# HGRN2 heads on one Trainium2 core: eight strip products in four runs of two levels instead of three runs of three, two and three

## The chip, the core and the metric

The kernel runs on one core of one Trainium2 chip. The core has a matmul engine (PE; its weight loads are shown as an engine of their own, PEld), three other computing engines (DVE, ACT, POOL), a queue engine (SP), an on-chip memory, and PSUM, eight banks into which PE writes and from which DVE and ACT read. Each engine works through its instructions in order and waits on semaphores for the others. The metric is the device time in microseconds (us) of one execution; three were run, and their median is the time before.

## What is computed

A backbone of two layers over 1024 latent tokens and 256 context tokens, width 1024, float32. The first layer (neighbourhood attention beside an mLSTM) is not touched. The second has 16 bidirectional HGRN2 heads with key and value width 128. Cut to what matters here, a head computes, in each direction:

```python
def step(S, xs):
    qc, kc, vc, lfc = xs
    b = jnp.cumsum(lfc, axis=2)
    o = jnp.einsum('bhtk,bhkv->bhtv', qc * jnp.exp(b), S)
    pair = jnp.exp(jnp.where(tri, b[:, :, :, None, :] - b[:, :, None, :, :], -jnp.inf))
    a = jnp.einsum('bhtk,bhtsk->bhts', qc, pair * kc[:, :, None, :, :])
    o = o + jnp.einsum('bhts,bhsv->bhtv', a, vc)
    ...
    S = jnp.exp(bL[:, :, 0])[..., None] * S + jnp.einsum('bhsk,bhsv->bhkv', kc * jnp.exp(bL - b), vc)
    return S, o
```

Here q = silu(projection), f = lb + (1 - lb) * sigmoid(projection) for each direction, k = 1 - f and lf = log(f); the state S starts from the context tokens. The outputs of the two directions are added, normalised, gated and projected.

## The kernel before

**A head.** The 1024 tokens are cut into 8 chunks of 128. Within a chunk the scores a (128 x 128, both directions at once, `gA`) are not computed with the decay between every pair of tokens, but in levels. Level 0 to 6 pairs neighbouring blocks of h = 1, 2, 4 ... 64 tokens. K (`gK`) and Q (`gQ`), both 128 x 2 x 1024, start as 1 - f and q * f, and after each level `hg_update` (line 1299) multiplies half of each in place with the block totals (`gT`), four DVE instructions of 128 x 512 at L1312, so that K is decayed to the border of the next larger block and Q from it; L1315 forms the next totals. The product of a level is thus a plain matmul, of which only the places that belong to the level are kept. One more level, called None, is the diagonal: (K0 + K1) against q.

**Strips.** `hg_level` (line 1276) computes a level as 32 products: for each of 8 chunks and 4 strips of 32 rows, 32 x 32 results (level 6: 32 x 64) on a quarter of the matmul array (`tile_position=(0, r)`, line 1295). Each call makes two matmuls and two weight loads in the trace, so a level is 64 matmul rows. `hg_pick` (line 1260) is a copy on ACT that gathers every other block of K or Q into a contiguous `gksel` tile (four buffers); where a level does not pick Q, the strips read Q in place through a strided view.

**Runs.** `hg_burst` (line 1266) issues a list of levels. It raises their priority by 3000, and binds each further level behind the first matmul of the first one (`issue_after`, which adds an order on one engine). Nothing binds the first level: it goes as soon as its operands and banks allow. The runs are (1, 0, None), then (3, 2), then (6, 4, 5): 192, 128 and 192 matmuls. DVE merges levels 0, None and 1 to 4 into `gA32` (L1215, and masked copies at L1214), ACT copies `gA32`, level 5 and level 6 into `gA` (L1237 to L1240).

**The order of the work.** The instruction order of each engine is planned when the kernel is built, by priority (order of the program text) and by when operands and banks are free in a planned time line. In the program text, `hg_intra` (line 1179) for head h has eight slots, filled by the loop at lines 1633 to 1646: the scan of head h-1 (`hg_scan`, line 1318: `back` in slots 0 to 2, `ahead` in slots 3 to 6), the projections of head h+1 (`hg_parts`, line 821: f of direction 0 in slots 2 and 3, of direction 1 in 4 and 5, q in 6 and 7), its context state (`hg_ctx`, slot 1), the load of v and the output of head h-2. A projection of 512 tokens is 24 matmuls of 128 x 512 (lines 127 to 129, `dense`), into one of two `mm` banks that ACT empties.

**Banks.** In this stage PSUM has `mm` (2), `tr` (2, transposes), `s` (3) and `acc` (1). The strips and the state matmuls both use `s`: each of a head's 14 states (L1327, read by DVE at L1329) and two context states (L1173, read by DVE at L1175) takes a tile there, and so does each pair of levels (level 6 and level 1 one each).

## Time and profile before

| | |
|---|---|
| three runs | 3323.93 us median, 3320.77 to 3324.95 |
| the profiled execution | 3323.42 us, its span 3321.6 us |
| PE busy | 3265.4 us (98%), 29504 matmuls |
| DVE, ACT, POOL busy | 2201.2, 1551.6, 499.4 us |
| the HGRN2 heads | first strip matmul at 2200.7 us, last at 3167.9 us |
| strip matmuls (L1295) | 8192 |

The profile is one execution, recorded by the hardware. A row names the source line, the engine, the operation, what is written and read by the program's names, and the shape. Matmuls overlap, and the end of one is modelled: start to start is the true pace, and a row's duration is longer. Idle time before an instruction is put down to what released it; "issue" means that the profile shows nothing that it waited for. The granted clock is the share of its full clock that PE was allowed.

### The profile page before, as it was taken

The page shows a single profiled execution, that of the slowest core. Times are in us where ns is not written, and L with a number is a line of the kernel's source. Part 1 is how long each engine was busy: PE and PEld are TensorE (multiplying, and loading weights), DVE is VectorE, ACT ScalarE, POOL GpSimd, SP SyncE. Part 2 cuts the span into 40 slices and gives each one's busy share as a digit, 9 for nine tenths or more (in the row PEclk, how much of TensorE's full clock was granted, in tenths as well). Part 3 has the DMA queues.
Part 4 walks back from the last instruction along what each step waited for, and adds up shares of the span by engine and source line. Part 5 has one row for each costly group of instructions (what it writes and reads, how often), then busy time and mean ns, then how long its engine had stood idle before and what let it go on. Part 6 is the DMA issues. An engine that isn't in the chain of part 4 may idle for free. (4 is left out here: it accounts for less than half of the span.)

```text
span 3321.6 us, 73610 instructions
## 1 busy us (share of the span) xinstructions
PE 3265.4 (98%) x29504; PEld 2909.4 (88%) x29504; DVE 2201.2 (66%) x5071; ACT 1551.6 (47%) x3469; POOL 499.4 (15%) x834
## 2 busy tenths in 40 slices
PE   8999999999999999999999999999999999999999
PEld 5689999999999999888877999888888888888887
DVE  5578747766667654666767766657767767767745
ACT  5322145555455534556645433355555555555541
POOL 3111112222222211121222111100000000000010
PEclk9999999999999999999999999999999999999999
DMA  8543322322232224455567333221122122122345
GB/s 270 199 140 103 120 80 55 95 74 80 77 84 79 80 89 134 142 169 155 153 196 225 115 105 108 91 66 55 56 65 62 56 65 65 53 65 65 119 159 171
DMA packets 359559, 360.36 MB, mean 108 GB/s; under 512 B 30584, under 2 KB 304184, under 8 KB 359088
## 3 DMA queue, kind: packets, MB, share of 16 engines
q1 hardware_dynamic: 315248, 246.36, 25.3%
q0 software_dynamic: 43824, 109.16, 9.7%
q8 instruction: 232, 3.80, 0.5%
q14 instruction: 111, 0.91, 0.1%
q10 hardware_dynamic: 144, 0.13, 0.0%
HBM read 271.98 MB, written 83.42 MB: 107 GB/s over the span
## 5 line engine op out<-in xcount | busy, mean ns | idle before, releaser
L127 PE MATMUL mm<-hh,wh 128*128 128x512 f32 (+1 forms) x1564 | 568.6, 364 | 0.1
L129 PE MATMUL mm<-hh,wl 128*128 128x512 f32 (+1 forms) x1564 | 561.7, 360 | 1.8 <-DVE wl L75 1.8
L128 PE MATMUL mm<-hl,wh 128*128 128x512 f32 (+1 forms) x1564 | 562.1, 359 | 0.0
L127 PE MATMUL mm<-wh,hh 128*128 128x256 f32 x1880 | 541.6, 289 | 3.7 <-ACT wh L74 3.6
L128 PE MATMUL mm<-wl,hh 128*128 128x256 f32 x1880 | 541.9, 289 | 0.1
L129 PE MATMUL mm<-wh,hl 128*128 128x256 f32 x1880 | 541.8, 289 | 0.2 <-DVE hl L75 0.2
L127 PEld LDWEIGHTS mm<-wh,hh 128*128 128x128 f32 x1880 | 358.0, 191 | 6.2 <-ACT wh L74 3.8
L128 PEld LDWEIGHTS mm<-wl,hh 128*128 128x128 f32 x1880 | 358.5, 191 | 3.6 <-issue 1.7
L129 PEld LDWEIGHTS mm<-wh,hl 128*128 128x128 f32 x1880 | 358.4, 191 | 3.3 <-issue 1.5
L127 PEld LDWEIGHTS mm<-hh,wh 128*128 128x128 f32 x1564 | 296.6, 190 | 43.3 <-issue 4.2
L129 PEld LDWEIGHTS mm<-hh,wl 128*128 128x128 f32 x1564 | 295.9, 189 | 43.3 <-DVE wl L75 2.0
L128 PEld LDWEIGHTS mm<-hl,wh 128*128 128x128 f32 x1564 | 296.7, 190 | 42.1 <-issue 4.2
L74 ACT CAST wh<-wraw 128x512 fp32r<-128x512 f32 x292 | 177.9, 620 | 209.9 <-PE mm L128 97.2
L75 DVE TENSOR_TENSOR wl<-wraw,wh 128x512 fp32r<-128x512 f32 x292 | 197.7, 687 | 84.2 <-ACT wh L74 69.8
L774 PE MATMUL mm<-woh,yh 128*128 128x512 f32 (+1 forms) x420 | 167.8, 399 | 4.1 <-ACT yh L74 3.1
L776 PE MATMUL mm<-woh,yl 128*128 128x512 f32 (+1 forms) x420 | 167.3, 399 | 0.5 <-DVE yl L75 0.4
L775 PE MATMUL mm<-wol,yh 128*128 128x512 f32 (+1 forms) x420 | 164.9, 393 | 0.0
L1312 DVE TENSOR_TENSOR gQ<-gQ,gT 128x512 f32<-128x512 f32 x192 | 123.9, 687 | 61.4 <-PE s L1295 60.3
L74 ACT CAST wh<-b 128x512 fp32r<-128x512 f32 x122 | 75.5, 620 | 178.6 <-PE sa L129 62.6
L1312 DVE TENSOR_TENSOR gK<-gK,gT 128x512 f32<-128x512 f32 x192 | 123.5, 685 | 12.3 <-PE s L1295 8.5
L1263 ACT COPY gksel<-gK 128x1024 f32<-128x1024 f32 x96 | 110.9, 1155 | 29.4 <-PE s L1295 15.1
L152 POOL TENSOR_SCALAR gss<-gss 128x4 f32<-128x4 f32 x32 | 12.9, 402 | 721.0 <-ACT gon L1353 721.0
(595 smaller groups left out, 7856.3 us busy)
## 6 DMA issues: line engine op xcount, KB each, us to landing
wraw<-in_wc_dram SPq DMA_DIRECT2D x130, 256.0 KB
wraw<-yd SPq DMA_DIRECT2D x116, 256.0 KB
wraw<-in_wab_dram SPq DMA_DIRECT2D x98, 256.0 KB
md<-ev POOLq DMA_DIRECT2D x78, 256.0 KB, 2.8
adar<-in_wada_dram POOLq DMA_DIRECT2D x16, 1024.0 KB, 5.9
b<-in_wc_dram SPq DMA_DIRECT2D x62, 256.0 KB
adar<-in_wada_dram SPq DMA_DIRECT2D x16, 512.0 KB
wraw<-in_wab_dram SPq DMA_DIRECT2D x64, 128.0 KB
```

Source lines behind the costliest of these rows:

```text
L74: nc.scalar.copy(hi, x)
L75: nc.vector.tensor_tensor(out=lo, in0=x, in1=hi.bitcast(F32), op=ALU.subtract)
L127: mm(ps, lhsT=lh(k), rhs=rh(k), start=(first and k == 0), stop=False)
L128: mm(ps, lhsT=lh(k), rhs=rl(k), start=False, stop=False)
L129: mm(ps, lhsT=ll(k), rhs=rh(k), start=False, stop=(last and k == nk - 1))
L152: g.tensor_scalar(out=out, in0=ssq, scalar1=mul, scalar2=EPS, op0=ALU.mult, op1=ALU.add)
L774: mm(ps, lhsT=yh[:, k, :], rhs=w.h(k)[:, cols], start=(k == 0), stop=False)
L775: mm(ps, lhsT=yh[:, k, :], rhs=w.l(k)[:, cols], start=False, stop=False)
L776: mm(ps, lhsT=yl[:, k, :], rhs=w.h(k)[:, cols], start=False, stop=(k == 7))
L1263: self.nc.scalar.copy(o.rearrange("p (b s i) -> p b s i", s=2, i=h), self.hg_view(t, h))
L1312: nc.vector.tensor_tensor(out=t[:, i, :, s, :], in0=t[:, i, :, s, :], in1=bc(tot), op=ALU.mult)
```

## The change

`hg_intra` issues four runs of two levels: (0, None) behind slot 2, (2, 1) behind slot 4, (4, 3) behind slot 6 and (6, 5) behind slot 7, so 128 matmuls each. Level 0's run no longer holds level 1, which was the only level of it that read Q in place; of the pairs (2, 1), (4, 3) and (6, 5) the first member reads Q in place (level 6 K too) and the second reads picked copies. Q is picked for levels 0, 1, 3 and 5 instead of 0, 2, 4 and 5, K for levels 0 to 5 as before. Slot 7 moves from behind the copies into `gA` to ahead of the last run. `dense` notes the last projection matmul written so far (`self.last_pe`), and `hg_burst` now binds the first level too: behind that matmul. The strips get a tile of their own, `sb`, of two banks and one buffer, and `s` shrinks from three banks to one, for the states alone.

```diff
--- before.py
+++ after.py
@@ -126,7 +126,7 @@
         for k in range(nk):
             mm(ps, lhsT=lh(k), rhs=rh(k), start=(first and k == 0), stop=False)
             mm(ps, lhsT=lh(k), rhs=rl(k), start=False, stop=False)
-            mm(ps, lhsT=ll(k), rhs=rh(k), start=False, stop=(last and k == nk - 1))
+            self.last_pe = mm(ps, lhsT=ll(k), rhs=rh(k), start=False, stop=(last and k == nk - 1))
 
 
     def proj_nat(self, ps, w, tt, c0, n, k0=0, nk=KD):
@@ -1192,53 +1192,58 @@
             for part in slots[i]:
                 part()
 
-        def two(w=32):
-            ps = self.ps("s", [P, 512])
-            return [ps[:, i : i + 8 * w].rearrange("p (c i) -> p c i", i=w) for i in range(0, 512, 8 * w)]
-
+        def banks(n):
+            ps = self.t(self.pp, [P, 1024], F32, "sb")
+            return [ps[:, i : i + 256].rearrange("p (c i) -> p c i", i=32) for i in range(0, n * 256, 256)], ps[:, 512:]
+
+        bc = lambda m: m.unsqueeze(1).to_broadcast([P, 8, 32])
+        put = lambda lev, ps: nc.vector.copy_predicated(A32, bc(self.lmask[:, lev - 1, :]), ps)
+        pick = lambda t, lev: self.hg_pick(t, lev, pool)
         slot(0)
-        k0, q0 = self.hg_pick(K, 0, pool), self.hg_pick(Q, 0, pool)
+        k0, q0 = pick(K, 0), pick(Q, 0)
         ks = self.hg_tile(pool)
         nc.vector.tensor_tensor(out=ks, in0=K[:, 0, :], in1=K[:, 1, :], op=ALU.add)
         self.hg_update(H, 0, pool)
-        k1 = self.hg_pick(K, 1, pool)
+        k1 = pick(K, 1)
         slot(1)
         slot(2)
-        (p0, pd), (p1, _) = two(), two()
-        self.hg_burst([(1, p1, k1, Q), (0, p0, k0, q0), (None, pd, ks, q)])
+        (p0, pd), _ = banks(2)
+        self.hg_burst([(0, p0, k0, q0), (None, pd, ks, q)])
+        q1 = pick(Q, 1)
         self.hg_update(H, 1, pool)
-        k2, q2 = self.hg_pick(K, 2, pool), self.hg_pick(Q, 2, pool)
-        self.hg_update(H, 2, pool)
-        k3 = self.hg_pick(K, 3, pool)
-        bc = lambda m: m.unsqueeze(1).to_broadcast([P, 8, 32])
-        put = lambda m, ps: nc.vector.copy_predicated(A32, bc(m), ps)
+        k2 = pick(K, 2)
         nc.vector.tensor_tensor(out=A32, in0=p0, in1=bc(self.lmask0), op=ALU.mult)
-        put(self.ident8, pd)
-        put(self.lmask[:, 0, :], p1)
+        nc.vector.copy_predicated(A32, bc(self.ident8), pd)
         slot(3)
         slot(4)
-        p2, p3 = two()
-        self.hg_burst([(3, p3, k3, Q), (2, p2, k2, q2)])
+        (p1, p2), _ = banks(2)
+        self.hg_burst([(2, p2, k2, Q), (1, p1, k1, q1)])
+        self.hg_update(H, 2, pool)
+        k3, q3 = pick(K, 3), pick(Q, 3)
         self.hg_update(H, 3, pool)
-        k4, q4 = self.hg_pick(K, 4, pool), self.hg_pick(Q, 4, pool)
-        self.hg_update(H, 4, pool)
-        k5, q5 = self.hg_pick(K, 5, pool), self.hg_pick(Q, 5, pool)
-        self.hg_update(H, 5, pool)
-        put(self.lmask[:, 1, :], p2)
-        put(self.lmask[:, 2, :], p3)
+        k4 = pick(K, 4)
+        put(1, p1)
+        put(2, p2)
         slot(5)
         slot(6)
-        (p4, p5), (p6,) = two(), two(64)
-        self.hg_burst([(6, p6, K, Q), (4, p4, k4, q4), (5, p5, k5, q5)])
+        (p3, p4), _ = banks(2)
+        self.hg_burst([(4, p4, k4, Q), (3, p3, k3, q3)])
+        self.hg_update(H, 4, pool)
+        k5, q5 = pick(K, 5), pick(Q, 5)
+        self.hg_update(H, 5, pool)
+        put(3, p3)
+        put(4, p4)
+        slot(7)
+        (p5,), p6 = banks(1)
+        p6 = p6.rearrange("p (c i) -> p c i", i=64)
+        self.hg_burst([(6, p6, K, Q), (5, p5, k5, q5)])
         self.hg_update(H, 6, pool)
-        put(self.lmask[:, 3, :], p4)
         for r in range(0, P, 32):
             s, o = slice(r, r + 32), r ^ 32
             nc.scalar.copy(A[s, :, s], A32[s])
             nc.scalar.copy(A[s, :, o : o + 32], p5[s])
         for r in (0, 64):
             nc.scalar.copy(A[r : r + 64, :, 64 - r : 128 - r], p6[r : r + 64])
-        slot(7)
         H["kn"] = {}
         for hf in (1, 0):
             for d in range(2):
@@ -1265,12 +1270,12 @@
 
     def hg_burst(self, todo):
         tc = self.tc
-        first, p = None, tc.cur_priority
+        first, p = self.last_pe, tc.cur_priority
         tc.cur_priority = p - 3000
         for lev, ps, k, q in todo:
-            with tc.issue_after(first.ins) if first else nullcontext():
+            with tc.issue_after(first.ins):
                 m = self.hg_level(lev, ps, k, q)
-            first = first or m
+            first = m if first is self.last_pe else first
         tc.cur_priority = p
 
     def hg_level(self, lev, ps, k, q):
@@ -1625,7 +1630,7 @@
                 self.rawp = pool
                 self.zero = self.t(pool, [P, CTX], F32, "gzero", 1)
                 nc.vector.memset(self.zero, 0.0)
-                l1.enter_context(self.pp.phase(s=3, acc=1))
+                l1.enter_context(self.pp.phase(s=1, sb=(1, 2), acc=1))
                 st, parts = self.hg_parts(0, pool, early)
                 for part in sum(parts, []):
                     part()
@@ -1720,7 +1725,7 @@
     @contextmanager
     def phase(self, **tags):
         with self.tc.tile_pool(name="ps" + "".join(tags), bufs=1, space=PSUM) as pool:
-            self.inner = {t: (pool, n) for t, n in tags.items()}
+            self.inner = {t: (pool, n if isinstance(n, int) else n[0]) for t, n in tags.items()}
             yield
         self.inner = {}
```

## The prediction

> **What bounds the kernel now.** I read the page first (engines, clock, queues), then the busy time stretch by stretch from one head's first strip run to the next, then PE's rows in order of time, then the waits.

> ```profile
> span 3321.6 us, 73610 instructions
> PE 3265.4 (98%) x29504; PEld 2909.4 (88%) x29504; DVE 2201.2 (66%) x5071; ACT 1551.6 (47%) x3469; POOL 499.4 (15%) x834
> q8 instruction: 232, 3.80, 0.5%
> ```

> PE is busy 98% of the span, so only time in which PE stands, or PE work itself, is worth anything. The third line is a DMA queue that carries instructions: 3.80 MB in 232 packets, 16.4 KB each. PE's two rows count 59,008 instructions; over 232 packets that is 254 a packet. So PE's program is brought in by blocks of some 255 instructions, about 128 pairs of a weight load and a matmul.

> Now the HGRN2 heads. Each stretch runs from the first strip run of a head to that of the next (columns: length, then busy time and instructions of PE, PEld, DVE, ACT, POOL, granted clock, DMA share, GB/s).

> ```profile
> 2316.58:2380.78 64.20, 62.00 (x843) 54.60 (x843) 43.64 (x83) 32.60 (x64) 4.01 (x6) 0.97 0.20 59
> 2380.78:2441.17 60.39, 60.39 (x843) 53.09 (x842) 43.20 (x83) 32.63 (x64) 4.05 (x6) 1.00 0.21 63
> 2441.17:2502.24 61.07, 60.59 (x843) 53.18 (x843) 43.29 (x83) 32.70 (x64) 4.04 (x6) 1.00 0.21 62
> 2502.24:2566.88 64.64, 62.14 (x843) 54.58 (x843) 43.62 (x83) 32.62 (x64) 4.02 (x6) 0.97 0.19 55
> 2627.27:2689.99 62.72, 60.59 (x843) 53.19 (x842) 43.41 (x83) 32.61 (x64) 4.05 (x6) 1.00 0.20 61
> 2750.39:2812.69 62.30, 60.57 (x843) 53.18 (x842) 43.43 (x83) 32.61 (x64) 4.02 (x6) 1.00 0.21 61
> 2812.69:2875.09 62.40, 60.56 (x843) 53.17 (x842) 43.45 (x83) 32.62 (x64) 4.02 (x6) 1.00 0.20 61
> 2935.49:2998.07 62.58, 60.59 (x844) 53.19 (x843) 43.40 (x83) 32.62 (x64) 4.04 (x6) 1.00 0.20 61
> 2998.07:3058.46 60.39, 60.39 (x843) 53.11 (x843) 43.23 (x83) 32.63 (x64) 4.05 (x6) 1.00 0.21 63
> ```

> The same 843 matmuls take 60.39 us in some heads, with PE busy throughout, and 61 to 65 us in others. A clean head leaves PE no idle time and DVE and ACT much (43 and 33 of 60 us). What the others lose is in PE's rows (start, duration, name, count, and in brackets the idle time before it and what ended it):

> ```profile
> 2320.38 0.65 PE L1295 MATMUL s<-gq,gksel 128*32 128x32 f32 x31 [2.20 <-issue]
> 2443.06 0.67 PE L1295 MATMUL s<-gq,gksel 128*32 128x32 f32 x54 [0.48 <-issue]
> 2506.60 0.22 PE L1295 MATMUL s<-gq,gksel 128*32 128x32 f32 x1 [2.50 <-issue]
> 2631.09 0.40 PE L1295 MATMUL s<-gq,gksel 128*32 128x32 f32 x24 [2.13 <-issue]
> 2753.57 0.62 PE L1295 MATMUL s<-gq,gksel 128*32 128x32 f32 x47 [1.73 <-issue]
> 2817.17 0.27 PE L1327 MATMUL s<-gv,gkn 128*128 128x128 f32 x1 [1.84 <-issue]
> 2939.21 0.35 PE L1295 MATMUL s<-gq,gksel 128*32 128x32 f32 x18 [1.99 <-issue]
> 3062.35 0.57 PE L1295 MATMUL s<-gq,gksel 128*32 128x32 f32 x41 [2.38 <-issue]
> 3133.82 0.38 PE L1346 MATMUL acc<-gS,gQ 128*128 128x128 f32 x1 [1.71 <-issue]
> ```

> Nine stops, ended by "issue": no semaphore explains them, and PE has no others of that kind between 2190 and 3200 us. Seven lie in the last third of a head's first strip run (the level that reads gq, matmuls 129 to 192 of it), two a few matmuls behind that run. Where they lie is regular: 31 matmuls are left after the stop in one head and 54 two heads later; 1, 24, 47 in heads two apart; 18 and 41. That is 23 a step. A head holds 843 + 842 = 1685 instructions with rows; two heads 3370 = 13 blocks of 256 + 42, or 21 pairs, and 23 if each head has two instructions without rows. So I read each stop as PE reaching the edge of a block that has not come yet.

> **Part by part: the runs.** Two runs of the old kernel, with what surrounds them:

> ```profile
> 2405.18 0.39 PE L127 MATMUL mm<-hh,wh 128*128 128x512 f32 x1
> 2405.41 0.39 PE L128 MATMUL mm<-hl,wh 128*128 128x512 f32 x1
> 2405.73 1.10 PE L1295 MATMUL s<-gQ,gK 128*32 128x64 f32 x64
> 2406.76 0.49 PE L1345 MATMUL acc<-gv,gA 128*128 128x128 f32 x2
> 2407.08 0.39 PE L1346 MATMUL acc<-gS,gQ 128*128 128x128 f32 x2
> 2407.31 0.39 PE L1347 MATMUL acc<-gS,gQ 128*128 128x128 f32 x2
> ...
> 2413.90 0.39 PE L128 MATMUL mm<-hl,wh 128*128 128x512 f32 x1
> 2414.21 1.30 PE L1295 MATMUL s<-gksel,gksel 128*32 128x32 f32 x128
> 2415.44 0.49 PE L1347 MATMUL acc<-gS,gQ 128*128 128x128 f32 x2
> ```

> A projection matmul starts 0.23 us after the one before, a pair on acc takes 0.23, but 128 strip matmuls pass in 1.23 us, under 10 ns each. A block whose 128 pairs all lie inside a strip run is used up in 1.2 us. By the stops, fetching one takes longer: 1.2 us plus a stop of up to 2.5, so some 3.5 to 4 us, with one block fetched ahead. A run of 192 can hold a whole block for 64 of 128 alignments, and a few more where the edge falls just behind it: nine of sixteen heads stopped. A run of 128 can hold a whole block at one alignment only; else part of the block is projections or acc pairs, of which ten to twenty add the missing 2.5 us. The old kernel shows it: its second run (128) in sixteen heads and, in all but the first head, its last (128) make 31 runs, at alignments that go round in steps of 23 pairs per two heads, and none has a stop. The change makes all four runs 128.

> What is removed: seven heads above exceed 60.39 by 3.81, 0.68, 4.25, 2.33, 1.91, 2.01 and 2.19 us, 17.2 in all. In two of them the granted clock is 0.97, and the head loses some 1.5 us more than the stop: PE was slowed after it. The last two heads run beside output matmuls, so I take their stops, 2.38 and 1.71 plus 0.2 each (by which the excess of 2.33 or 2.19 stands above the idle time shown, 2.13 and 1.99): 4.5. Sum 21.7 us.

> What is added: a run costs 0.09 us at its entry (0.32 instead of 0.23 from the matmul before) and about 0.25 at its end (the 64 above take 1.03 us, 0.15 more than 63 steps of 14 ns; the acc pair behind them 0.32 instead of 0.23). But in fifteen heads the old third run (64 + 128) came apart, as shown, so they have four runs already. Only the first head gains one: 0.3 us. In all 21.4 us are gained.

> **The other parts.** The number of strip matmuls, picks, updates, masked copies and states is the same; q1 and q3 are picked instead of q2 and q4, ten picks a head as before, on ACT, which has 27 us a head to spare. The first run no longer reads Q in place, so the second update need not wait for it:

> ```profile
> DVE gQ L1312 <- PE s L1295: 60.3, 16, 4.3
> DVE gS L1329 <- PE s L1327: 37.8, 50, 2.3
> PEld s L1295 <- DVE gS L1329: 0.4, 1, 0.4
> ```

> That wait of DVE, 3.8 us a head, is cover and no cost: PE was busy beside it. I take nothing for it. A fixed place moves runs later than their operands allow; then DVE's updates wait longer, with 17 us a head to spare. If that is used up, PE would stand at the next run. Slot 7, now ahead of the last run, holds 24 projection matmuls (5.5 us at 0.23), the sigmoid and product behind them on ACT and DVE, and the last two chunks on acc with their squares on ACT and their root on POOL; it issues no DMA (q's weights are fetched from slot 6). So update 6, the copies into gA and the next states come up to 5.5 us later; the next head's context and f projections (24 matmuls of 0.12 and 24 of 0.23, 8.4 us) cover that, and without them it would cost 5.5 us a head. I take zero.

> The disputed part is the state matmul's bank. "s" shrinks from three banks to one, and sixteen tiles a head (fourteen states, two context states) pass through it, each held until DVE has read it:

> ```profile
> 2423.62 0.83 PE L1327 MATMUL s<-gv,gkn 128*128 128x128 f32 x6
> 2430.73 0.34 DVE L1329 SCALAR_TENSOR_TENSOR gS<-gS,gT,s 128x128 f32<-128x128 f32 x1
> 2440.62 0.38 PE L1327 MATMUL s<-gv,gkn 128*128 128x128 f32 x2
> 2441.04 0.35 DVE L1329 SCALAR_TENSOR_TENSOR gS<-gS,gT,s 128x128 f32<-128x128 f32 x1 [0.87 <-PE s L1327]
> ```

> The first two rows: three states go out at once and the last is read 7 us later; that needs three banks. The last two: one tile from start to free in 0.77 us. Sixteen at 0.77 take 12 of 60 us, so one bank suffices if DVE answers soon. Behind a waiting state matmul PE's whole queue stands. Bounds: nothing, if projections are always placed between two states, as around 2440; or 0.77 - 0.23 = 0.54 us for each of 16 x 16 tiles, 138 us, if they follow each other bare. The nearest row is the third wait above: in this stage PE waited for a state's reading once, 0.4 us, though the banks were shared with the strips. The order is planned with these waits, so I take the lower end, zero, and keep up to 0.5 us a head (8 us) in the range. Nothing below zero: a clean head has no idle PE to win.

> Sum: 3323.4 us of the profiled execution (its span of 3321.6 and 1.8 around it) - 21.7 + 0.3 = 3302.0; the median of the three runs (3323.9) is 0.5 above that execution: I forecast 3302.5.

> **Rivals.** *Slower: the single bank.* PE's matmuls stand behind a state whose bank DVE has not read, because DVE is inside an update:

> ```profile
> L1312 DVE TENSOR_TENSOR gQ<-gQ,gT 128x512 f32<-128x512 f32 x192 | 123.9, 687 | 61.4 <-PE s L1295 60.3
> ```

> Twelve of them a head, 0.69 us each. Break-even is 21.4/16 = 1.3 us a head, two such waits; with four of sixteen tiles waiting 0.69 us it is 2.8 us a head, 44 in all: 3323.9 - 21.4 + 44 = 3347. For it: DVE answered up to 7 us late. Against it: no PE wait on DVE now, projections at hand everywhere. Chance 0.13.

> *No change: the stops are not the runs' length.* If the blocks come late for another reason, the stops move to other places and remain: 3324. [...] Against this rival stands that PE's other runs, of 128 and less, never stop this way. Chance 0.09.

> *Half the gain: a run of 128 may fall just on a block.* Four runs in sixteen heads are 64; if one in eight is aligned so and loses 1.3 us, 10 us come back: 3313. Chance 0.1.

> **How the numbers follow.** The forecast has 0.68, the half gain 0.1, no change 0.09, the bank 0.13. A measurement of this kernel can tell about 0.2%, 6.6 us. Faster by more than that: 0.68 and nearly all of the 0.1, less a little for waits of the bank that eat the gain: 0.76. Within: 0.11. Slower: 0.13. The forecast's own range is 3297 to 3311: below, if the reordered end also loses this wait for the first output matmul (2 us, and 1.5 for a slower clock behind it), less 2 us for the scatter of runs (3320.8 to 3325.0);

> ```profile
> 3107.93 0.50 PE L774 MATMUL mm<-wh,yh 128*128 128x512 f32 x1 [2.07 <-ACT yh L74]
> ```

> above, with 0.5 us a head for the bank. To leave out no more than 2 in 10 the range reaches over the half gain and no change: 3297 to 3325.

> **What would show it.** Right: every head some 60.4 us apart, no idle time ended by "issue" at L1295 or just behind, four rows x128 a head (one of them 64 + 64 where widths differ), granted clock 1.00 throughout. Wrong: "issue" stops inside runs of 128 (the half gain), or as many elsewhere (no change); "PE s L1327 <- DVE gS L1329" among the waits with more than 20 us (the bank); runs split into 64s, at 0.3 us each.

## The result, and the profile after

The changed kernel takes 3442.05 us (median of four, 3439.7 to 3448.3) against 3324.4 for the kernel before: a ratio of 1.0362, with an interval of 1.035 to 1.0375 (the two medians alone give 1.0354). It is slower by 118 us, where 21 us less were forecast. The page of the changed kernel:

```profile
span 3441.9 us, 73572 instructions
PE 3324.7 (97%) x29504; PEld 2959.2 (86%) x29504; DVE 2209.4 (64%) x5071; ACT 1551.1 (45%) x3469; POOL 507.8 (15%) x834
core 0: 3441.9 us, clock 0.976
```

The last of these lines (from the view of cores) is the mean granted clock, 0.995 before. The span is 120 us longer. PE's matmuls are the same 29504, but PE stands 117 us instead of 56 (span less busy time), and is busy 59 us longer with the same work. Both arise from the first strip run on: behind it PE stands 86 us instead of 24, and ahead of it about as long as before (31.5 and 32.5 us). Two heads, from first strip run to first strip run, and then one border between heads cut in three (columns as in the prediction):

```profile
2664.35:2733.76 69.41, 65.17 (x842) 56.80 (x842) 43.73 (x82) 32.60 (x63) 4.64 (x7) 0.92 0.18 54
2733.76:2804.39 70.63, 65.28 (x842) 57.35 (x842) 43.76 (x82) 32.71 (x63) 4.64 (x7) 0.91 0.18 54
...
2588.60:2592.00 3.40, 1.27 (x8) 0.94 (x6) 2.32 (x3) 3.33 (x13) 0.44 (x1) 1.00 0.56 185
2592.00:2605.60 13.60, 10.70 (x165) 9.97 (x166) 11.52 (x23) 8.88 (x13) 2.82 (x3) 0.50 0.12 43
2605.60:2611.00 5.40, 5.40 (x26) 4.50 (x25) 2.46 (x5) 1.36 (x3) 0.00 (x0) 0.99 0.47 141
```

From the fourth head to the fourteenth a head takes 69 to 71 us instead of 60.39; in the two shown PE idles 4 to 5 us and is busy 5 us longer. The lower rows show why it is busy longer: for 13.6 us at a border where PE stood, the granted clock was 0.50. PE's rows at that border:

```profile
2589.48 0.39 PE L1332 MATMUL s<-gv,gkn 128*128 128x128 f32 x2
2592.36 0.80 PE L1332 MATMUL s<-gv,gkn 128*128 128x128 f32 x2 [2.49 <-DVE gS L1334]
2593.66 1.08 PE L1300 MATMUL sb<-gksel,gksel 128*32 128x32 f32 x64 [0.51 <-ACT gksel L1268]
2594.54 1.06 PE L1300 MATMUL sb<-gq,gksel 128*32 128x32 f32 x64
2595.63 0.80 PE L1332 MATMUL s<-gv,gkn 128*128 128x128 f32 x2
2596.22 1.06 PE L1376 MATMUL tr<-ident,gon 128*128 128x128 f32 x4
2597.07 0.63 PE L1350 MATMUL acc<-gv,gA 128*128 128x128 f32 x2
2599.72 0.58 PE L127 MATMUL mm<-hh,wh 128*128 128x256 f32 x1 [2.01 <-ACT gF L839]
2600.10 0.41 PE L128 MATMUL mm<-hl,wh 128*128 128x256 f32 x1
2600.31 0.41 PE L129 MATMUL mm<-hh,wl 128*128 128x256 f32 x1
```

Two state matmuls follow each other, and the second waits until DVE has read the first one's bank. The first run then waits for ACT's pick of Q, and the projection behind it for ACT to empty a bank of mm. The last rows show the slow clock: a step of 0.21 us for a 128x256 matmul that takes 0.12 at full clock. The first run follows 4.2 us after the first state matmul; in a clean head of the kernel before PE had no idle time there. What DVE and ACT did meanwhile:

```profile
2589.68 2.36 DVE L1186 TENSOR_TENSOR gQ<-gq,gF 128x1024 f32<-128x1024 f32 x2 [1.55 <-PE acc L1352]
2591.96 0.34 DVE L1334 SCALAR_TENSOR_TENSOR gS<-gSc,gT,s 128x128 f32<-128x128 f32 x1
...
2586.71 0.41 ACT L1243 COPY gA<-gA 32x256 f32<-32x256 f32 x1 [3.76 <-PE acc L1350]
2592.09 1.52 ACT L1268 COPY gksel<-gQ 128x1024 f32<-128x1024 f32 x1
2598.02 1.15 ACT L1268 COPY gksel<-gK 128x1024 f32<-128x1024 f32 x1 [4.41 <-DVE gK L1317]
2599.07 0.59 ACT L839 ACTIVATE gF<-mm 128x512 f32<-128x512 f32 x1
```

DVE was in the two products that form Q, 2.36 us together, and only then read the state. These products had themselves waited for the last acc matmuls of the head before, which read the old Q. ACT had stood 3.76 us until acc matmuls of that head had read gA, of which there is one buffer, so its ten copies into gA came that much later. But the pick of Q that the run waited for started 0.05 us after the products were done, so it could hardly have gone earlier even without that delay. The next pick waited for DVE's update of K, and the emptying of mm stood behind it in ACT's order. The waits of the stage (the first row is DVE's own idle time; a row for PE and one for PEld can be the same wait):

```profile
DVE gS L1334 <- PE s L1332: 174.7, 89, 4.9
PEld s L1332 <- DVE gS L1334: 48.0, 34, 3.1
PE s L1332 <- DVE gS L1334: 41.5, 24, 2.9
PE mm L127 <- ACT gF L839: 16.6, 13, 2.9
PE sb L1300 <- ACT gksel L1268: 12.8, 15, 2.2
PEld sb L1300 <- issue: 12.1, 34, 0.4
```

The third row is the one that the prediction named for its slower rival, "more than 20 us". The last shows the other half of the prediction at work: no stop by "issue" at a strip run is longer than 0.4 us, where nine of 0.5 to 2.5 us stood in or just behind the runs before.

### The profile page after: what moved, and what is told of

Its sections match the earlier page's. It is cut to its first block, busy times and chain, and to the rows that moved or that the text cites. A ratio compares the mean times of both kernels' runs of the same rounds, so it can differ in the third digit from the quotient of the medians.

```text
span 3441.9 us, 73572 instructions
## 1 busy us (share of the span) xinstructions
PE 3324.7 (97%) x29504; PEld 2959.2 (86%) x29504; DVE 2209.4 (64%) x5071; ACT 1551.1 (45%) x3469; POOL 507.8 (15%) x834
## 4 chain that ended last, share of the span: by engine, by line
PE 43%; ACT 3%; DVE 1%; DMA 1%; issue 1%; POOL 1%; SPq 0%; POOLq 0%; ACTq 0%
PE mm L127 7%; PE mm L128 7%; PE mm L129 7%; PE mm L774 2%; PE mm L776 2%; PE mm L775 2%; PE sb L1300 2%; PE sa L128 2%; PE sa L129 2%; PE sa L127 2%; PE s L1332 1%; PE acc L1351 1%; PE acc L1352 1%; PE tr L1253 1%; PE acc L1350 1%
## 5 line engine op out<-in xcount | busy, mean ns | idle before, releaser
L127 PE MATMUL mm<-hh,wh 128*128 128x512 f32 (+1 forms) x1564 | 584.2, 374 | 16.7 <-ACT gF L839 16.6
L129 PE MATMUL mm<-hh,wl 128*128 128x512 f32 (+1 forms) x1564 | 572.8, 367 | 1.8 <-DVE wl L75 1.8
L128 PE MATMUL mm<-hl,wh 128*128 128x512 f32 (+1 forms) x1564 | 569.3, 364 | 0.0
L127 PE MATMUL mm<-wh,hh 128*128 128x256 f32 x1880 | 542.4, 289 | 2.9 <-ACT wh L74 2.9
L128 PE MATMUL mm<-wl,hh 128*128 128x256 f32 x1880 | 542.9, 289 | 0.0
L127 PEld LDWEIGHTS mm<-wh,hh 128*128 128x128 f32 x1880 | 358.9, 191 | 5.4 <-ACT wh L74 3.1
L128 PEld LDWEIGHTS mm<-wl,hh 128*128 128x128 f32 x1880 | 359.5, 191 | 3.5 <-issue 1.7
L127 PEld LDWEIGHTS mm<-hh,wh 128*128 128x128 f32 x1564 | 308.0, 197 | 60.8 <-ACT gF L839 19.9
L129 PEld LDWEIGHTS mm<-hh,wl 128*128 128x128 f32 x1564 | 305.8, 196 | 43.9 <-DVE wl L75 2.0
L128 PEld LDWEIGHTS mm<-hl,wh 128*128 128x128 f32 x1564 | 307.6, 197 | 40.4 <-issue 4.2
L74 ACT CAST wh<-wraw 128x512 fp32r<-128x512 f32 x292 | 178.9, 619 | 220.8 <-PE mm L128 106.0
L1334 DVE SCALAR_TENSOR_TENSOR gS<-gS,gT,s 128x128 f32<-128x128 f32 x192 | 66.0, 344 | 175.1 <-PE s L1332 173.6
L774 PE MATMUL mm<-woh,yh 128*128 128x512 f32 (+1 forms) x420 | 169.0, 402 | 5.1 <-ACT yh L74 4.3
L74 ACT CAST wh<-b 128x512 fp32r<-128x512 f32 x122 | 75.5, 620 | 178.4 <-PE sa L129 62.6
L1317 DVE TENSOR_TENSOR gK<-gK,gT 128x512 f32<-128x512 f32 x192 | 123.9, 686 | 30.3 <-ACT gksel L1268 27.8
L1332 PE MATMUL s<-gv,gkn 128*128 128x128 f32 x448 | 98.2, 303 | 42.7 <-DVE gS L1334 42.4
```

The lines of the kernel that those rows point to most:

```text
L74: nc.scalar.copy(hi, x)
L127: mm(ps, lhsT=lh(k), rhs=rh(k), start=(first and k == 0), stop=False)
L128: mm(ps, lhsT=lh(k), rhs=rl(k), start=False, stop=False)
L129: self.last_pe = mm(ps, lhsT=ll(k), rhs=rh(k), start=False, stop=(last and k == nk - 1))
L774: mm(ps, lhsT=yh[:, k, :], rhs=w.h(k)[:, cols], start=(k == 0), stop=False)
L1317: nc.vector.tensor_tensor(out=t[:, i, :, s, :], in0=t[:, i, :, s, :], in1=bc(tot), op=ALU.mult)
```

## The experiments

**Runs and banks apart.** My theory after the result: the single bank of the states is the whole loss, and the four runs do what was forecast. Rivals: the fixed places, or the new order of runs and slot 7. Four kernels take the change apart. The first two keep the new runs and give the states more banks. The banks have to come from somewhere: in the first the strips' tile shrinks from two banks to one (level 6 takes a tile of `s`), in the second strips and states share three.

```diff
-            ps = self.t(self.pp, [P, 1024], F32, "sb")
+            ps = self.t(self.pp, [P, 512], F32, "sb")
+            p6 = self.ps("s", [P, 512]) if n == 1 else None
...
-                l1.enter_context(self.pp.phase(s=1, sb=(1, 2), acc=1))
+                l1.enter_context(self.pp.phase(s=2, sb=1, acc=1))
```

> The changed kernel, but the strips get one bank (level 6 takes a tile of s) and the states two. Theory bank (the states' single bank holds PE behind DVE, the scan ends late, PE runs dry at each head's border and its clock is halved there): at least three quarters of the 118 us go, and the stops of before stay away, so 3300 to 3335 us, PE's waits for DVE at the states under 10 us in all. Rival place (runs bound behind projections come late): about 3440. Rival runs (the order of updates and slot 7): about 3440.

It took 3309.7 us, a ratio to before of 0.9966 (0.9953 to 0.9979). Its heads, its clock and its waits:

```profile
2313.35:2373.82 60.47, 60.47 (x844) 53.22 (x843) 42.96 (x83) 32.63 (x64) 3.59 (x6) 1.00 0.21 63
2978.48:3038.95 60.47, 60.47 (x844) 53.21 (x843) 42.96 (x83) 32.69 (x64) 3.59 (x6) 1.00 0.21 63
...
core 0: 3305.1 us, clock 0.996
...
PE s L1333 <- DVE gS L1335: 0.3, 1, 0.3
PEld sb L1301 <- issue: 9.9, 32, 0.4
```

From the third head on every head is clean, PE waits for a state once, and PE has no stop by "issue" left at the strips. One bank more for the states, with one less for the strips, takes away 0.0396 of the time before, 132 us. Between the two profiled executions, whose runs are the same, PE idles 76 us less and is busy 61 us less.

```diff
-            ps = self.t(self.pp, [P, 1024], F32, "sb")
+            ps = self.ps("s", [P, 512])
+            p6 = self.ps("s", [P, 512]) if n == 1 else None
...
-                l1.enter_context(self.pp.phase(s=1, sb=(1, 2), acc=1))
+                l1.enter_context(self.pp.phase(s=3, acc=1))
```

> The changed kernel, but strips and states share three banks s, as before the change. Theory bank: 3300 to 3335 us. Rivals place and runs: about 3440.

3312.2 us, 0.9971 (0.9958 to 0.9983): the new runs with the old banks are as good, within what can be told. The third does the opposite, old runs with the new banks:

```diff
-        (p0, pd), (p1, _) = two(), two()
+        (p0, pd, p1), _ = banks()
...
-        p2, p3 = two()
+        (p2, p3, _), _ = banks()
...
-        (p4, p5), (p6,) = two(), two(64)
+        (p4, p5, _), p6 = banks()
...
-                l1.enter_context(self.pp.phase(s=3, acc=1))
+                l1.enter_context(self.pp.phase(s=1, sb=1, acc=1))
```

> The kernel before, with its three runs, but the new banks: two for the strips, one for the states. Theory bank: slow, 3400 us or more, with PE waiting for DVE at the states by 40 us or more in all; the nine stops of the fetch may remain. Rivals place and runs: 3324, as before.

3468.0 us, 1.044 (1.0416 to 1.0464): 146 us slower than before with no change of the runs. The strips' tile changes here too, so not all of the 146 us need be the states' bank. Its clock and PE's waits:

```profile
core 0: 3465.3 us, clock 0.978
...
PE s L1328 <- DVE gS L1330: 55.5, 35, 2.9
PE sb L1296 <- DVE gQ L1313: 30.2, 13, 2.5
PE sb L1296 <- issue: 21.3, 14, 2.1
```

Here both losses stand side by side: the waits for the states, and in the last row fourteen stops by "issue", 1.5 us on the mean, which the old runs of 192 still have. In the middle row strips wait for DVE's update of Q, a wait that PE's rows of the kernel before do not have. The fourth is the changed kernel without the fixed places:

```diff
-        first, p = self.last_pe, tc.cur_priority
+        first, p = None, tc.cur_priority
...
-            with tc.issue_after(first.ins):
+            with tc.issue_after(first.ins) if first else nullcontext():
```

> The changed kernel with the first level of each run not bound behind the projections. Theory bank: about 3440, at least 3410. Rival place: 3300 to 3335.

3427.8 us, 1.0319 (1.0296 to 1.0343). The places cost 14 us while the states have one bank, but they are not the loss. So the bank is shown as its cause, in both orders of runs, and both rivals fall. The strips' tile is not the cause either: it has one buffer in the two-bank version too, and in the changed kernel PE never waits for the reading of it. But one row of this kernel speaks against the forecast that runs of 128 do not stop:

```profile
PE sb L1300 <- issue: 3.2, 3, 1.3
```

Three of its 64 runs of 128 stopped by "issue", for 1.10, 0.74 and 1.35 us, behind matmul 120, 127 and 108 of the run.

**Place and slot 7 with two banks.** The same edit of `hg_burst`, made to the two-bank version, and then, in a kernel of its own, slot 7 put back behind the copies into gA:

> The two-bank version without binding the first level behind the projections. Theory bank (with two banks for the states PE always has other work, wherever the runs lie): within 6 us of the two-bank version, 3304 to 3316. Rival (the fixed places keep PE fed): slower by 15 us or more, with idle time of PE at the heads' borders.

3308.0 us, 0.9954 (0.9936 to 0.9971).

```diff
-        slot(7)
...
+        slot(7)
```

> The two-bank version with slot 7 back behind the copies into gA, as in the kernel before, so that the last run follows the one before with no projections of slot 7 between. Theory bank: within 6 us of the two-bank version, 3304 to 3316. Rival (the late update 6 costs, as the prediction bounded it at up to 5.5 us a head): faster by 10 us or more.

3308.9 us, 0.9957 (0.9942 to 0.9971). Neither can be told from the two-bank version. All three are faster than the kernel before, by 0.3 to 0.5%, with intervals that do not reach 1. In the version with slot 7 last, PE stopped by "issue" twice a few matmuls behind a run of 128, for 0.62 and 1.34 us.

**Is it the length of a run?** In the two-bank version the first run's two levels were computed twice, 256 matmuls in a row:

```diff
-        self.hg_burst([(0, p0, k0, q0), (None, pd, ks, q)])
+        self.hg_burst([(0, p0, k0, q0), (None, pd, ks, q)] * 2)
```

> The two-bank version (new runs, s two banks, strips one) with the first run's two levels computed twice in a row, to the same values: 256 matmuls instead of 128. Theory fetch (a run that holds a whole block of 256 instructions outruns the fetching of the next): every one of the sixteen heads stops by issue for some 2 us at about the same depth behind a block's edge; 18 us of added work and 30 to 40 us of stops on top of 3310, so 3355 to 3370. Rival (the stops of before had nothing to do with the length of a run): the added work alone, 3328, and no stops.

3375.1 us, 1.0156 (1.0136 to 1.0176), 5 us beyond the upper end of what the fetch theory expected. PE's wait and its clock, and the stop in the first and in the fifth head:

```profile
PE sb L1301 <- issue: 34.2, 16, 2.7
...
core 0: 3375.9 us, clock 0.993
...
2205.49 0.64 PE L1301 MATMUL sb<-gksel,gksel 128*32 128x32 f32 x29 [2.26 <-issue]
...
2460.90 0.36 PE L1301 MATMUL sb<-gksel,gksel 128*32 128x32 f32 x20 [1.92 <-issue]
```

Sixteen heads, sixteen stops, 2.1 us on the mean, all in the doubled run and none in the 48 runs of 128 beside it; four more stops, of 0.2 to 1.2 us, came at other matmuls behind it. With 128 pairs to a block a run of 256 holds a whole block at every alignment, and every one stopped: in the first head behind matmul 161 of the run, in the fifth behind 169.

Then the old kernel with None moved out of its first run:

```diff
-        (p0, pd), (p1, _) = two(), two()
-        self.hg_burst([(1, p1, k1, Q), (0, p0, k0, q0), (None, pd, ks, q)])
+        p0, p1 = two()
+        self.hg_burst([(1, p1, k1, Q), (0, p0, k0, q0)])
...
         slot(3)
+        pd, _ = two()
+        with tc.issue_after(self.last_pe.ins):
+            self.hg_burst([(None, pd, ks, q)])
+        put(self.ident8, pd)
```

> The kernel before with the level None taken out of the first run and issued behind the projections of slot 3, as a run of 64 of its own; banks as before (s three, shared). Theory fetch: the nine stops go and nothing else changes but one more run a head (0.35 us): 3303 to 3312. Rival (stops not due to the run's length): 3322 to 3330 with stops elsewhere.

3316.4 us, 0.998 (0.9969 to 0.999): 7 us gained, where 11 to 20 were expected. The old last run (6, 4, 5), which came apart into 64 and 128 in fifteen heads, now went out whole in all sixteen, and six of these runs of 192 stopped in place of the first run; one of them, and the wait as the view of waits sums it:

```profile
2290.18 0.55 PE L1298 MATMUL s<-gksel,gksel 128*32 128x32 f32 x24 [2.41 <-issue]
...
PE s L1298 <- issue: 10.5, 6, 2.4
```

My expectation missed that the edit makes another long run. The stops went where the 192 went, as the fetch theory has it. Why the last run is whole here is not shown.

**Why one bank costs so much.** Two theories for how waits of 42 us come to more than 130. First, the clock. Twelve matmuls that nothing needs were put between the two state matmuls of the border:

```diff
+        (p0, pd), spare = banks(2)
+        at, pr = self.last_pe, self.tc.cur_priority
+        self.tc.cur_priority = pr - 3000
+        with self.tc.issue_after(at.ins):
+            for i in range(12):
+                self.last_pe = nc.tensor.matmul(
+                    spare, lhsT=self.hh[:, i % 8, 0:P], rhs=self.hh[:, i % 8, 0:512], start=True, stop=True
+                )
```

> The changed kernel with twelve matmuls of 128x512 more per head, whose results nothing reads, written into the strips' second bank; they stand in PE's order between the two state matmuls at the head's border, where PE waited some 2.5 us for DVE (12 x 0.23 = 2.8 us of work, 44 us in sixteen heads). Theory clock (half of the loss is the halved clock that follows PE's idle time): the added work falls into the wait and the clock is halved in fewer windows, so faster than the changed kernel in spite of more work, 3385 to 3430. Rival (the halved clock does not follow from these waits): 3440 to 3490.

3433.5 us, 1.0337 (1.0307 to 1.0367): some 9 us faster than the changed kernel by the medians, with 44 us more of work. The intervals overlap, so no more can be told than that the added work cost no time; and it is 3 us outside the range expected of the clock theory. Its clock, its PE and its longest wait:

```profile
core 0: 3431.6 us, clock 0.989
PE 3334.0 (97%) x29696; PEld 2966.6 (86%) x29696; DVE 2213.2 (64%) x5071; ACT 1555.9 (45%) x3469; POOL 500.3 (15%) x834
PE sb L1215 <- ACT gA L1254: 44.6, 14, 3.2
```

The clock lost falls from 83 us (0.024 of 3441.9) to 38 (0.011 of 3431.6). Most of the idle time stayed, 98 us in all instead of 117: the added matmuls had to wait for ACT's copies to release their own bank, 44.6 us, in place of the waits for the states (42.4 us in the changed kernel, 3.1 here). So PE still stood at the border, 3.2 us at a time, but was loaded without a gap behind it, and two thirds of the extra slow time went. At the border shown above, the clock of 0.50 lasts 3.4 us here instead of 13.6. That the slow clock comes with these waits is shown, since it is gone in the two-bank version too; which pattern of load would avoid it wholly is not.

Second, the chain over gA. To make room for a second buffer of it, 4 KB a partition had to be freed, so there is a control:

```diff
-                self.zero = self.t(pool, [P, CTX], F32, "gzero", 1)
+                self.zero, self.rawb = self.t(pool, [P, 1], F32, "gzero", 1), 2
...
-        vT = self.t(pool, [P, CTX], F32, "gvT", 1)
+        vT = self.t(pool, [P, 2, CTX], F32, "gEc", 1)[:, 0, :]
...
-                raw = [pool, 3, "wraw"]
+                raw = [pool, 2, "wraw"]
```

> Control for the next: the changed kernel with 4 KB a partition freed (two raw weight buffers instead of three in this stage, a zero read as one broadcast element, the context's transposed v in the tile of its decays). All theories: within 12 us of the changed kernel, 3430 to 3455.

3440.5 us, 1.0358 (1.0327 to 1.0388), and PE's waits:

```profile
PE s L1332 <- DVE gS L1334: 50.9, 30, 2.9
PE sb L1300 <- ACT gksel L1268: 12.5, 15, 2.5
```

With the second buffer on top:

```diff
-        A = self.t(pool, [P, 8, P], F32, "gA", 1)
+        A = self.t(pool, [P, 8, P], F32, "gA", 2)
```

> The control with two buffers of gA instead of one, so that ACT's copies into gA need not wait for the last acc matmuls of the head before. Theory chain (the late scan holds ACT at those copies, ACT brings the next head's picks and the emptying of mm late, and PE waits for these): 30 us or more faster than the control. Rival (PE's waits for the states' bank are the cost by themselves): within 15 us of the control.

3422.2 us, 1.0303 (1.0273 to 1.0332), 18 us faster than the control: more than the rival allowed and less than the chain theory asked. PE's waits in it:

```profile
PE s L1332 <- DVE gS L1334: 42.0, 24, 2.9
PE sb L1300 <- ACT gksel L1268: 10.3, 15, 1.0
```

The second buffer is worth some 18 us, but not by the path of the chain theory. PE's waits for ACT hardly changed against the control (from 12.5 to 10.3 us, and from 4.6 to 4.9 for the emptying of mm); the wait for the states got shorter, from 50.9 to 42.0, and the clock lost fell from 72 us to 62. The wait for the states, with the clock behind it, is the larger part of the loss. How the rest divides is left open.

## Why the prediction was wrong, point by point

- *PE bounds the heads, and a clean one takes 60.39 us.* Right: 60.47 in the two-bank version, with PE busy throughout.
- *The stops are the fetch of the next block, outrun by long strip runs, and runs of 128 do not stop.* Right in the changed kernel: none longer than 0.4 us in its 64 runs, sixteen of sixteen at 256, 2.1 us on the mean, and stops that moved with the 192. That they are waits for the next block is inferred from this, from the step of 23 and from the instruction queue: in the kernel before one packet of 16.4 KB starts 2.2 to 3.0 us ahead of the end of each of the nine stops (the view of DMA by windows), 1 to 248 rows of PE and PEld ahead of it in eight of them and 282 in the other, so with PE in the block before or 26 rows short of it: one block ahead, as the estimate of 3.5 to 4 us had it. Which instructions a packet holds is not shown. The rival "no change" falls. That a run of 128 can stop, as "half the gain" has it, is seen in the kernel without places, three times in 64, 3.2 us in all, and twice just behind a run in the version with slot 7 last; in the changed kernel it did not happen.
- *The runs gain 21.4 us.* With enough banks they gain 0.0034 of 3322 us, 11 us (7 to 16), or 15 (10 to 21) without places; the profiled executions are 16.5 and 18.4 us shorter. The term was sized too high, at nearly twice the 11 us, and not for the reason of "half the gain", since no stop is left in that version. The heads' pace explains 1.3 us of it (0.08 us in sixteen heads); the rest is not settled.
- *The states' bank: "I take the lower end, zero".* This is the step that failed. It measured 132 us with the new runs and 146 with the old. That this is about the upper bound of 138 is luck: the bound lets every one of 256 tiles wait 0.54 us, whereas PE waited for a state 26 times, 1.6 us on the mean, and the rest came from the waits for ACT behind it and from the clock. My evidence was a row of 0.4 us, a strip run's wait in the kernel before for a bank that held a state. But that row was measured with three banks, where the planned order could let a state lie 7 us unread. It could not speak of one bank. A row that did speak was in the prediction, a state read 7 us late; the products of 2.36 us in front of the read were not. I also argued that the order is planned with such waits in mind. At the border shown that did not help: projections were not at hand, since both mm banks were full until ACT emptied them at 2599.07 and 2600.63.
- *The rival "single bank".* Right in kind, with the row that it named; its price of 44 us was a third of what it measured. It counted waits of 0.69 us behind one update, where the border's waits are 2.5, 0.5 and 2 us, and it left out the clock: against the two-bank version 76 us more of idle time came with 61 us more of busy time.
- *Moved slot 7, places, the second update's wait, ten picks: zero.* Right with two banks for slot 7 and the places (3308.9 and 3308.0 us against 3309.7). With one bank the places cost 14 us. The update's wait and the picks were not tested by themselves.

## What to carry to other kernels

A row that shows a resource without waits says nothing of the kernel in which that resource is cut to a third; count how long each tile is held (from the writer's start to the reader's end), and what its reader has in front of it, and price the tail of that, not the shortest case. When PE is the bound, price the slower work around its idle time too: here 76 us of idle time, in gaps such as 2.5, 0.5 and 2.0 us at one border, came with 61 us of slower work at a lower granted clock (0.976 against 0.996). And keep a run of short instructions well below the length that stops: here 256 pairs stopped in every head, 192 in nine of sixteen, and 128 in three runs of 64 in one kernel and in none in the changed one.

## What the runs showed of the hardware

A stop ended by "issue" in a run of 256 lasts 2.1 us on the mean of sixteen. With runs of 192 the old kernel stopped in nine heads of sixteen, with the same code in each; the matmuls left after a stop moved by 23 in two heads. Between the stops that ended at 2320.38 and 2443.06 us lie 3322 rows of PE and PEld, 13 times 255.5. Between 2200 and 3200 us there are 26,905 such rows, and the instruction queue (q8) started 105 packets: 256 rows a packet. Both fit blocks of 256 instructions.
